# The state-space branch of a decoder trunk: its drive for two state tiles at a time in plain float32, its read-out for four

## The chip, the cores and the metric

The kernel runs on one core of a Trainium2 chip. The metric is the device time of one launch in microseconds (us), as the median of several runs. Engines are named as in the profile: PE is TensorE's matmul stream and PEld its weight loads, DVE is VectorE, ACT is ScalarE, POOL is GpSimd, SP issues the weight DMAs.

## What is computed

Two layers of a decoder trunk on 256 tokens of width 1024, all in float32. Each layer is a SwiGLU feed-forward half step, a mixing step and a second feed-forward half step. The mixing step projects the normed input once; its columns go to a sliding-window attention (3 groups of 8 heads) and to a state-space branch of width 512 (32 groups of 16 channels, 64 complex states a group). Cut to that branch:

```python
u = u.reshape(Bsz, S, SSM_GROUPS, SSM_GROUP)
bu_re = jnp.einsum('bsgc,gpc->bsgp', u, bb_re)      # the drive
bu_im = jnp.einsum('bsgc,gpc->bsgp', u, bb_im)
...
_, _, xr, xi = lax.associative_scan(combine, (ar, ai, bu_re, bu_im), axis=1)
y = (jnp.einsum('bsgp,gcp->bsgc', xr, c_re) - jnp.einsum('bsgp,gcp->bsgc', xi, c_im)
     + d_skip * u)                                   # the read-out and the skip
y = jax.nn.gelu(y.reshape(Bsz, S, SSM_WIDTH))
ga, gb = jnp.split(y @ w_glu, 2, axis=-1)
return ga * jax.nn.sigmoid(gb)
```

## The kernel before

**Weights.** Every large product is done in float32r, in three products of halves: `mm3` (lines 200 to 203) multiplies the high half of a weight (`whi`) with the low and the high half of the data, and its low half (`wlo`) with the high half of the data. The weights come from memory as plain float32 in units of 2048 columns (`raw`, a ring of four, read by SP as a place comes free). `split_one` makes the halves: a cast on ACT (L163) and a subtraction on DVE (L164), up to seven half units ahead of PE (`NHB`). Units of the modulation's weights are spread among them and are multiplied and summed on DVE (L247).

**The mixing step** (`mix_sub`) runs these products in order: a first block of six column tiles; queries and keys for head pairs (`qk`), values (`v`), gates (`gt`), the attention's projection (`ap`), the state-space branch's last projection (`ga`, `gb`), the output (`mo`). After each column tile `tock` runs the work that is due in that slot of a table (`at`): small pieces of attention (logits `lg`, transposes `pt`, outputs `po`) and of the state-space branch. They stand between the large matmuls on PE.

**The state-space branch.** A layer has 16 state tiles of 128 states; four tiles (a quad, `q`) share 128 channels of u, and each tile reads 32 of them. For tile s at its slot m:

- `ssm_in` (slot m - 1), the drive: real and imaginary part, each in three float32r products over 32 rows of the array (`bh` with `ul`, `bh` with `uh`, `bl` with `uh`), 256 columns each, six matmuls into one PSUM bank (`bu`). The row group is 32 times (s mod 4).
- `ssm_turn` (slot m) and `ssm_scan` (m + 1): nine DVE instructions that turn the drive by a table (`tab`), scan it twice over time and turn it back into `xs`.
- `ssm_out` (slot m + 3 of an odd tile), the read-out of tiles s - 1 and s: plain float32, two matmuls a tile (`cw` with `xs`), each tile in its own group of 32 columns, into the bank `yps` of the quad, which is taken with the quad's first pair.
- after a quad: `ssm_skip` adds `d_skip` times u in two DVE steps (for `uh` and `ul`), `ssm_gelu` and `ssm_low` make the halves for the last projection.

Ahead of this, `split_act` makes the halves `bh` and `bl` of B, and `uh`, `ul` are made from the first block's tiles.

**Order.** SP, POOL and ACT run in the order of the code. In the mixing step, behind its first block, PE and DVE are ordered by the framework's scheduler, which moves pieces by its own estimate of when their inputs are ready. All PSUM tiles come from one pool of eight banks (`bank`).

Of the kernel before, what the change touches and what calls it, by code (L numbers as in the profile page):

```python
# [10 lines left out]
F32 = mybir.dt.float32  # L11
# [9 lines left out]
S = 256  # L21
# [42 lines left out]
def plan_units():  # L64
    """Order in which the units of weights are read: ('w', i) or ('a', i)."""
# [22 lines left out]
def ada_chunks(gi):  # L88
    """(layer, chunk of 1024 columns) of the modulation made in group gi."""
# [13 lines left out]
def trunk(ctx, tc, xT, cv, par, ssmp, cst, emat, tbl, wada, wpk, bmat, cmat, out):  # L103
# [37 lines left out]
    def take_ada():  # L141
        """Modulation units whose turn it is."""
# [42 lines left out]
    def several(n):  # L185
        """Halves that are read together."""
# [48 lines left out]
    def ada_unit():  # L235
        """256 columns of silu(c) @ w_ada, one column per partition and element."""
# [57 lines left out]
    def soon(fn):  # L294
        """fn, with its instructions ahead of those that are emitted up to SOON earlier."""
# [16 lines left out]
    def rstd_start():  # L312
        """1 / sqrt(mean of squares + eps), tokens on partitions."""
# [17 lines left out]
    def rstd_spread(ys):  # L331
        """The same on every partition, in PSUM."""
# [169 lines left out]
    def table_side(l, pool):  # L502
        """Cosine and sine of each state's angle over time, for the scans of layer l."""
# [27 lines left out]
    def gate_of(sub):  # L531
        """Half the gate."""
# [71 lines left out]
    def first_block(nx, sj, rj):  # L604
        """Five column tiles of a sublayer's input projection. They read scale * x; the rest read the
        normed chunks, which are made meanwhile. What comes back: the banks, 1 / rms, the normed chunks."""
# [44 lines left out]
    def first_block_whole(nx, sub):  # L651
        """The same for four column tiles, in plain float32."""
        scale, shift, z = nx
        us = [("w", first[sub] + j) for j in range(2)]
        ws = [raw.pop(u).rearrange("p (a b) -> p a b", b=128) for u in us]
        look()
        pss = [bank("b1") for _ in range(4)]

        def mms(ks):
            for j in range(4):  # L660
                for k in ks:
                    T.matmul(pss[j][:, :S + 2], lhsT=ws[j // 2][:, 8 * (j % 2) + k, :], rhs=z[:, k, :],
                             start=k == 0, stop=k == KC - 1)
                if ks[0] == 0 and j == 1:
                    stat_mm()
                    stat["ys"] = rstd_start()
                if ks[0] > 0 and j % 2:
                    finish(us[j // 2])
                    take_ada()

        mms(range(5))
        rps = rstd_spread(stat["ys"])
        rs = tmp.tile([128, S], F32, name="rs", tag="sqa", bufs=1)
        A.copy(out=rs, in_=rps)
        hh, hl = [], []
        for k in h_tiles(rs, scale, shift, hh, hl):
            pass
        mms(range(5, KC))
        look()
        return pss, rs, hh, hl  # L680

    def first_sublayer():
# [183 lines left out]
    def mix_sub(sub, l, nx, close):  # L866
# [5 lines left out]
        if 1:  # L872
# [107 lines left out]
            def ssm_out(s):  # L980
                """State tiles s - 1 and s into their channels."""
                q, jj = divmod(s, 4)
                if jj == 1:
                    yps[q] = bank("yps")
# [398 lines left out]
```

## Time and profile before

| | |
|---|---|
| median of 3 runs | 1366.13 us (1364.47 to 1367.0) |
| span of the profiled execution, first to last instruction | 1361.8 us |
| PE busy | 1322.1 us (97%) |
| DVE busy | 1098.3 us (81%) |
| ACT busy | 757.2 us (56%) |
| mean granted clock of TensorE | 0.993 of full speed |
| DMA | 321.60 MB, mean 236 GB/s |

The profiled execution has no time of its own beside its span; the median stands 4.3 us above it. A busy time is the share of the span in which the engine had an instruction under way. Matmuls overlap: a record lasts longer than the distance to the next one, so PE's work is read from starts, not from durations. One plain float32 matmul shows as two records. `x8` behind a timeline row means eight records of one group that were merged; the row then lasts from the first start to the last end.

### The profile page before, as it was taken

To read this page: it belongs to the slowest core of one execution; us is meant where nothing else is said; L and a number is where in the kernel's file an instruction comes from. 1 tells how busy PE (TensorE), PEld (TensorE's weight loads), DVE (VectorE), ACT (ScalarE), POOL (GpSimd) and SP (SyncE) were. 2 spreads that over 40 slices of the span, in tenths; PEclk is the share of its full clock that TensorE was granted. 3 is DMA by queue.
4 is the path that set the end of the run, shared out by engine and by line. 5 is a ranking of instruction groups with operands and counts; after the bars stand their busy time and mean duration, and the time that the engine had idled before them with its cause. 6 is when DMAs were issued, how large, how long until landed. Compare 5 with 4: busy or idle time off the path is not lost.

```text
span 1361.8 us, 26855 instructions
## 1 busy us (share of the span) xinstructions
PE 1322.1 (97%) x11018; PEld 1279.4 (94%) x11018; DVE 1098.3 (81%) x1757; ACT 757.2 (56%) x1162; POOL 292.6 (21%) x356
## 2 busy tenths in 40 slices
PE   4996999999999999999999999999999999999997
PEld 2996999998988999999999999999889999999997
DVE  8866997889899879998769888679889887876552
ACT  5634795645565456677646444454565645654441
POOL 5889691100000000877300000010000000000000
PEclk9997999999999999999999999999999999999999
DMA  9775997556665645998837988656555463586540
GB/s 356 297 289 175 369 347 274 187 193 207 219 234 219 217 153 170 347 370 321 279 124 291 351 316 333 247 174 227 173 199 198 163 220 128 182 307 217 186 155 32
DMA packets 48837, 321.60 MB, mean 236 GB/s; under 512 B 6048, under 2 KB 6432, under 8 KB 12746
## 3 DMA queue, kind: packets, MB, share of 16 engines
q1 hardware_dynamic: 41704, 296.24, 59.8%
q0 software_dynamic: 7008, 23.64, 5.4%
q8 instruction: 86, 1.41, 0.4%
q14 instruction: 37, 0.30, 0.1%
q10 hardware_dynamic: 2, 0.00, 0.0%
HBM read 310.38 MB, written 9.48 MB: 235 GB/s over the span
## 4 chain that ended last, share of the span: by engine, by line
PE 86%; POOL 6%; DVE 3%; issue 2%; ACT 1%; DMA 1%; DVEq 0%; POOLq 0%; ACTq 0%
PE pc L203 8%; PE pc L201 8%; PE pc L202 8%; PE fo L201 6%; PE fo L202 6%; PE fo L203 6%; PE qk L201 4%; PE qk L202 3%; PE qk L203 3%; PE gt L201 3%; PE gt L202 2%; PE gt L203 2%; PE b L201 2%; PE bu L949 2%; PE b L203 2%; PE b L202 2%
## 5 line engine op out<-in xcount | busy, mean ns | idle before, releaser
L164 DVE TENSOR_TENSOR wlo<-raw,whi 128x1024 fp32r<-128x1024 f32 x416 | 515.5, 1257 | 93.2 <-ACT whi L163 92.3
L163 ACT CAST whi<-raw 128x1024 fp32r<-128x1024 f32 x416 | 427.0, 1047 | 220.2 <-PE fo L202 71.3
L201 PE MATMUL pc<-hl,whi 128*128 128x256 f32 x1200 | 338.4, 282 | 8.7 <-ACT whi L163 8.7
L203 PE MATMUL pc<-hh,wlo 128*128 128x256 f32 x1200 | 338.2, 282 | 3.6 <-DVE wlo L164 3.6
L202 PE MATMUL pc<-hh,whi 128*128 128x256 f32 x1200 | 338.2, 282 | 0.0
L201 PEld LDWEIGHTS pc<-hl,whi 128*128 128x128 f32 x1200 | 226.6, 189 | 8.9 <-ACT whi L163 8.9
L203 PEld LDWEIGHTS pc<-hh,wlo 128*128 128x128 f32 x1200 | 226.5, 189 | 4.1 <-DVE wlo L164 4.1
L202 PEld LDWEIGHTS pc<-hh,whi 128*128 128x128 f32 x1200 | 226.7, 189 | 0.0
L201 PE MATMUL fo<-al,whi 128*128 128x256 f32 x704 | 197.7, 281 | 0.2 <-DVE al L341 0.2
L202 PE MATMUL fo<-ah,whi 128*128 128x256 f32 x704 | 197.8, 281 | 0.0
L203 PE MATMUL fo<-ah,wlo 128*128 128x256 f32 x704 | 197.7, 281 | 0.0
L247 DVE CUSTOM_DVE_ANT_0 raw<-raw,cb 128x1024 f32<-128x1024 f32 x144 | 182.2, 1300 | 7.4 <-DMA raw<-wada 7.1
L201 PEld LDWEIGHTS fo<-al,whi 128*128 128x128 f32 x704 | 132.6, 188 | 0.4 <-DVE al L341 0.4
L202 PEld LDWEIGHTS fo<-ah,whi 128*128 128x128 f32 x704 | 132.7, 188 | 0.0
L203 PEld LDWEIGHTS fo<-ah,wlo 128*128 128x128 f32 x704 | 132.7, 188 | 0.0
L201 PE MATMUL qk<-hl,whi 128*128 128x256 f32 x352 | 102.4, 292 | 0.0
L202 PE MATMUL qk<-hh,whi 128*128 128x256 f32 x352 | 99.1, 282 | 0.0
L203 PE MATMUL qk<-hh,wlo 128*128 128x256 f32 x352 | 98.7, 281 | 0.0
L389 POOL TENSOR_SCALAR tr<-tp 128x256 f32<-128x256 f32 x32 | 45.6, 1424 | 146.8 <-ACT tp L509 146.1
L883 POOL DMA_DIRECT2D tab<-tab x32 | 17.4, 545 | 267.8 <-DVE pq L276 171.3
L201 PE MATMUL gt<-hl,whi 128*128 128x256 f32 x256 | 74.7, 292 | 0.0
L201 PEld LDWEIGHTS qk<-hl,whi 128*128 128x128 f32 x352 | 66.1, 188 | 7.1 <-issue 4.7
(220 smaller groups left out, 2915.4 us busy)
## 6 DMA issues: line engine op xcount, KB each, us to landing
raw<-wpk SPq DMA_DIRECT2D x208, 1024.0 KB, 5.4
raw<-wada SPq DMA_DIRECT2D x72, 1024.0 KB, 6.8
tab<-tb POOLq DMA_DIRECT2D x32, 256.0 KB, 5.7
tab<-tab POOLq DMA_DIRECT2D x32, 256.0 KB, 3.6
bt<-wd POOLq DMA_DIRECT2D x8, 640.0 KB, 6.2
xt<-xT SPq DMA_DIRECT2D x1, 1024.0 KB, 4.9
bT<-bmat POOLq DMA_DIRECT2D x2, 512.0 KB, 4.8
out<-xt SPq DMA_DIRECT2D x4, 256.0 KB, 2.2
```

The costliest lines, as they stand in the source:

```text
L163: A.copy(out=hi.rearrange("p a b -> p (a b)"), in_=src)
L164: low.tensor_sub(out=lo.rearrange("p a b -> p (a b)"), in0=src, in1=hi.rearrange("p a b -> p (a b)"))
L201: T.matmul(ps, lhsT=wh, rhs=hl, start=start, stop=False)
L202: T.matmul(ps, lhsT=wh, rhs=hh, start=False, stop=False)
L203: T.matmul(ps, lhsT=wl, rhs=hh, start=False, stop=stop)
L247: V.tensor_tensor_reduce(out=wj, in0=wj, in1=cb, scale=1.0, scalar=0.0, op0=ALU.mult, op1=ALU.add, accum_out=m[:, c:c + 1])
L389: G.tensor_scalar(out=o, in0=i, scalar1=s1, scalar2=s2, op0=op0, op1=op1)
L883: G.dma_start(out=tabs[s], in_=tabd[l][s])
L949: T.matmul(ps[:, i * S:i * S + S], lhsT=w[r, i, q, :], rhs=u[q][r], start=n == 0, stop=n == 2, tile_position=(32 * jj, 0))
```

## The change

Four things change in `mix_sub`; nothing else does, but for a function that was never called (`first_block_whole`, since `NATIVE` is empty) and comments.

- B is kept in plain float32 (`bT`, a tile of its own), u too (`us`). The halves `bh`, `bl`, `ul` and what makes them are gone.
- The drive runs for tiles s and s + 1 together, at even s: one plain float32 matmul for each part and tile, the two tiles taking turns, so that the row group changes with every matmul. Each tile has its own bank.
- The read-out runs once a quad, at slot m + 3 of its last tile: eight plain float32 matmuls, the four tiles (column groups) taking turns. The scans' outputs `xs` have four buffers instead of two. The bank `yps` is taken only here.
- The skip is one DVE step instead of two.

```diff
-            bT = sp.tile([128, 1024], F32, name="bT", tag="pq", bufs=1)
-            bh, bl = (sp.tile([128, 2, 4, 128], F32R, name=n) for n in ("bh", "bl"))
-            G.dma_start(out=bT, in_=bmat[l].rearrange("p a b c -> p (a b c)"))
-            split_act(bT, bh.rearrange("p a b c -> p (a b c)"), bl.rearrange("p a b c -> p (a b c)"))
+            bT = sp.tile([128, 2, 4, 128], F32, name="bT")
+            G.dma_start(out=bT, in_=bmat[l])
...
                 t, c = first_out(pss.pop(0), rs)
-                a = sp.tile([128, S], F32R, name="uh", tag="uh", bufs=4)
-                b = sp.tile([128, S], F32R, name="ul", tag="ul", bufs=4)
...
-                stt(in_time(b), t, c, in_time(a), AD, SU)
+                a = sp.tile([128, S], F32, name="u", tag="uh", bufs=4)
+                A.activation(out=in_time(a), in_=t.rearrange("p (k m) -> p k m", k=2), func=AF.Identity, bias=c)
+                us.append(a)
...
             def ssm_in(s):
-                q, jj = divmod(s, 4)
-                ps = bank("bu")
-                r = slice(32 * jj, 32 * jj + 32)
+                for n in (s, s + 1):
+                    bus[n] = bank("bu")
                 for i in range(2):
-                    for n, (w, u) in enumerate(((bh, ul), (bh, uh), (bl, uh))):
-                        T.matmul(ps[:, i * S:i * S + S], lhsT=w[r, i, q, :], rhs=u[q][r], start=n == 0, stop=n == 2,
+                    for n in (s, s + 1):
+                        q, jj = divmod(n, 4)
+                        r = slice(32 * jj, 32 * jj + 32)
+                        T.matmul(bus[n][:, i * S:i * S + S], lhsT=bT[r, i, q, :], rhs=us[q][r], start=True, stop=True,
                                  tile_position=(32 * jj, 0))
...
-                x = sp.tile([128, 2, S], F32, name="xs", tag="xs", bufs=2)
+                x = sp.tile([128, 2, S], F32, name="xs", tag="xs", bufs=4)
...
-            def ssm_out(s):
-                q, jj = divmod(s, 4)
-                if jj == 1:
-                    yps[q] = bank("yps")
+            def ssm_out(q):
+                yps[q] = bank("yps")
                 for i in range(2):
-                    for j2 in (jj - 1, jj):
-                        T.matmul(yps[q][32 * j2:32 * j2 + 32, :S], lhsT=cw[:, i, 4 * q + j2, :],
...
+                    for jj in range(4):
+                        T.matmul(yps[q][32 * jj:32 * jj + 32, :S], lhsT=cw[:, i, 4 * q + jj, :],
+                                 rhs=prods[4 * q + jj][:, i], start=i == 0, stop=i == 1, tile_position=(0, 32 * jj))
...
-                stt(yys[q], uh[q], d, yps.pop(q)[:, :S], MU, AD)
-                stt(yys[q], ul[q], d, yys[q], MU, AD)
+                stt(yys[q], us[q], dskip[:, 4 * l + q:4 * l + q + 1], yps.pop(q)[:, :S], MU, AD)
...
-                at(m - 1, ssm_in, s)
+                if s % 2 == 0:
+                    at(m - 1, ssm_in, s)
...
-                if s % 2:
-                    at(m + 3, ssm_out, s)
                 if s % 4 == 3:
+                    at(m + 3, ssm_out, s // 4)
```

How this stands on the engines, in layer 0's mixing step. PE at the first drive, before (L201 to L203 are the large products of `qk`, L1113 to L1115 those of `v`):

```order
L203 MATMUL qk<-hh_3116,wlo 128x256
L949 MATMUL bu<-ul,bh 128x256
L949 MATMUL bu<-uh,bh 128x256
L949 MATMUL bu<-uh,bl 128x256
L949 MATMUL bu<-ul,bh 128x256
L949 MATMUL bu<-uh,bh 128x256
L949 MATMUL bu<-uh,bl 128x256
L1113 MATMUL v<-whi,hl_3034 128x256
```

and after, at the same place:

```order
L202 MATMUL qk<-hh_3116,whi 128x256
L203 MATMUL qk<-hh_3116,wlo 128x256
L913 MATMUL bu<-u,bT 128x256 x4
L1071 MATMUL v<-whi,hl_3034 128x256
L1072 MATMUL v<-whi,hh_3033 128x256
```

Six float32r matmuls of one tile became four plain ones of two tiles; the second tile's own six, 48 large matmuls later, are gone.

PE at a read-out of the first quad, before (one matmul of tile 2 alone, between two halves of the transposes `pt`):

```order
L203 MATMUL qk<-hh_3116,wlo 128x256
L1050 MATMUL pt<-cs,lg 128x128 x4
L987 MATMUL yps<-xs,cw 32x256
L1050 MATMUL pt<-cs,lg 128x128 x4
L1113 MATMUL v<-whi,hl_3034 128x256
```

and after, the read-out of the whole quad:

```order
L203 MATMUL qk<-hh_3116,wlo 128x256
L1008 MATMUL pt<-cs,lg 128x128 x8
L948 MATMUL yps<-xs,cw 32x256 x8
L1071 MATMUL v<-whi,hl_3034 128x256
L1072 MATMUL v<-whi,hh_3033 128x256
```

The quad's matmuls stood in five places on PE before and stand in one now. In each layer, the second quad's are the only ones that are cut, into 3, 2 and 3 by matmuls of `po`.

DVE ahead of the first drive, before (`fo`, `fb` take the first block's tiles out of PSUM):

```order
L276 TENSOR_TENSOR fo<-b_2922,rs 128x256
L787 COPY fb<-b_2922 128x1
L164 TENSOR_TENSOR wlo<-raw,whi 128x1024
L341 TENSOR_TENSOR bl<-bT,bh 128x1024
L279 SCALAR_TENSOR_TENSOR ul<-fo,fb,uh 128x2x128 x3
L276 TENSOR_TENSOR fo<-b_2923,rs 128x256
L787 COPY fb<-b_2923 128x1
```

and after:

```order
L276 TENSOR_TENSOR fo<-b_2922,rs 128x256
L756 COPY fb<-b_2922 128x1
L164 TENSOR_TENSOR wlo<-raw,whi 128x1024
L276 TENSOR_TENSOR fo<-b_2923,rs 128x256
L756 COPY fb<-b_2923 128x1
```

The low halves of B and of u are gone. Further on, DVE has made 123 low halves of weights by the end of the layer's last scan before and after, and 60 products of the modulation where there were 62; in layer 1 it has made 331 low halves where there were 330, and as many products.

## Rows read from the trace of the kernel before

**Rows 1.** the page: busy time, share of the span and instructions of each engine:

```profile
PE 1322.1 (97%) x11018; PEld 1279.4 (94%) x11018; DVE 1098.3 (81%) x1757; ACT 757.2 (56%) x1162; POOL 292.6 (21%) x356
```

**Rows 2.** busy time by stretch: from:to, length, engines' busy time, PEclk, DMA share, GB/s:

```profile
262.00:454.00 192.00, 191.92 (x1611) 174.45 (x1610) 177.26 (x319) 105.52 (x166) 10.95 (x17) 1.00 0.61 212
454.00:540.00 86.00, 86.00 (x715) 84.72 (x714) 69.25 (x134) 48.48 (x79) 0.00 (x0) 1.00 0.51 180
916.00:1107.00 191.00, 190.92 (x1620) 174.92 (x1619) 169.73 (x300) 107.82 (x169) 10.96 (x17) 1.00 0.57 196
```

**Rows 3.** waits of TensorE, longest first: total us, times, longest:

```profile
PE pc L201 <- ACT whi L163: 8.7, 1, 8.7
```

**Rows 4.** groups of instructions: xcount, busy us, mean ns, idle before:

```profile
L987 PE MATMUL yps<-xs,cw 128*32 128x256 f32 x128 | 22.0, 387 | 0.0
...
L949 PE MATMUL bu<-ul,bh 32*128 32x256 f32 x64 | 21.0, 328 | 0.0
```

**Rows 5.** timeline of TensorE around a drive: start, us, line, operation, tiles:

```profile
290.85 0.28 PE L203 MATMUL qk<-hh,wlo 128*128 128x256 f32 x1
291.06 0.38 PE L949 MATMUL bu<-ul,bh 32*128 32x256 f32 x1
...
292.19 0.27 PE L202 MATMUL qk<-hh,whi 128*128 128x256 f32 x1
```

**Rows 6.** timeline of TensorE around two read-outs, of one matmul and of four:

```profile
283.13 0.28 PE L1115 MATMUL v<-wlo,hh 128*128 128x256 f32 x1
283.34 0.62 PE L987 MATMUL yps<-xs,cw 128*32 128x256 f32 x2
...
284.11 0.29 PE L202 MATMUL qk<-hh,whi 128*128 128x256 f32 x1
...
335.06 0.28 PE L1115 MATMUL v<-wlo,hh 128*128 128x256 f32 x1
335.26 1.06 PE L987 MATMUL yps<-xs,cw 128*32 128x256 f32 x8
...
336.48 0.28 PE L202 MATMUL qk<-hh,whi 128*128 128x256 f32 x1
```

**Rows 7.** timeline of TensorE around the logits of a head pair:

```profile
286.73 0.28 PE L203 MATMUL qk<-hh,wlo 128*128 128x256 f32 x1
286.94 1.16 PE L1020 MATMUL lg<-qk 64*128 64x128 f32 x16
...
288.25 0.28 PE L202 MATMUL qk<-hh,whi 128*128 128x256 f32 x1
```

**Rows 8.** groups of instructions on VectorE:

```profile
L247 DVE CUSTOM_DVE_ANT_0 raw<-raw,cb 128x1024 f32<-128x1024 f32 x144 | 182.2, 1300 | 7.4 <-DMA raw<-wada 7.1
...
L279 DVE SCALAR_TENSOR_TENSOR ul<-fo,fb,uh 128x256 fp32r<-128x256 f32 x8 | 3.5, 480 | 0.0
...
L341 DVE TENSOR_TENSOR bl<-bT,bh 128x1024 fp32r<-128x1024 f32 x2 | 2.4, 1223 | 1.6 <-ACT bh L340 1.6
```

**Rows 9.** timelines of VectorE and TensorE at each layer's last scan and read-out:

```profile
452.37 0.75 DVE L276 TENSOR_TENSOR xs<-xs,pq 128x256 f32<-128x256 f32 x2
...
453.64 0.62 PE L987 MATMUL yps<-xs,cw 128*32 128x256 f32 x2
...
456.63 0.63 PE L987 MATMUL yps<-xs,cw 128*32 128x256 f32 x4
...
1101.65 0.75 DVE L276 TENSOR_TENSOR xs<-xs,pq 128x256 f32<-128x256 f32 x2
...
1106.54 1.06 PE L987 MATMUL yps<-xs,cw 128*32 128x256 f32 x8
```

**Rows 10.** waits of VectorE between 262 and 454 us:

```profile
DVE wlo L164 <- ACT whi L163: 3.9, 6, 1.3
DVE yl L1005 <- ACT yh L1001: 2.9, 2, 2.6
```

**Rows 11.** waits of VectorE between 916 and 1107 us:

```profile
DVE pq L276 <- PE bu L949: 6.3, 4, 2.5
```

More of the change, by code (lines that the diff above doesn't have):

```diff
@@ L649, in first_block @@
         return pss, rs, hh, hl
[L651 to L680, printed above, removed]
     def first_sublayer():
@@ L798, in ffn_sub @@
             with tc.manual_schedule(engines={E.PE}):
-                pss, rs, hh, hl = first_block_whole(nx, sub) if sub in NATIVE else first_block(nx, *(J2 if sub % 3 == 2 else J0))
+                pss, rs, hh, hl = first_block(nx, *(J2 if sub % 3 == 2 else J0))
         close()
@@ L867, in mix_sub @@
         with tc.manual_schedule(engines={E.PE}):
-            pss, rs, hh, hl = first_block_whole(nx, sub) if sub in NATIVE else first_block(nx, *(J2 if sub % 3 == 2 else J0))
+            pss, rs, hh, hl = first_block(nx, *(J2 if sub % 3 == 2 else J0))
         close()
@@ L893, in mix_sub @@
             load_bias(0)
-            cT = sp.tile([128, 2, 16, 16], F32, name="cT", tag="xs", bufs=2)
-            ct = sp.tile([128, 2, 16, 16], F32, name="ct", tag="xs", bufs=2)
+            cT = sp.tile([128, 2, 16, 16], F32, name="cT", tag="xs", bufs=4)
+            ct = sp.tile([128, 2, 16, 16], F32, name="ct", tag="xs", bufs=4)
             cw = sp.tile([128, 2, 16, 32], F32, name="cw")
@@ L915, in mix_sub @@
                 ctt(cw[r, 1, :, 16 * g:16 * g + 16], ct[r, 0], ct[r, 1], SU)
-            uh, ul, yh, yl = [], [], [], []
+            us, yh, yl = [], [], []
             for j in range(4):
                 t, c = first_out(pss.pop(0), rs)
-                a = sp.tile([128, S], F32R, name="uh", tag="uh", bufs=4)
-                b = sp.tile([128, S], F32R, name="ul", tag="ul", bufs=4)
-                t = t.rearrange("p (k m) -> p k m", k=2)
-                A.activation(out=in_time(a), in_=t, func=AF.Identity, bias=c)
-                stt(in_time(b), t, c, in_time(a), AD, SU)
-                uh.append(a)
-                ul.append(b)
+                a = sp.tile([128, S], F32, name="u", tag="uh", bufs=4)
+                A.activation(out=in_time(a), in_=t.rearrange("p (k m) -> p k m", k=2), func=AF.Identity, bias=c)
+                us.append(a)
             ev = {}
@@ L942, in ssm_in @@
             def ssm_in(s):
-                q, jj = divmod(s, 4)
-                ps = bank("bu")
-                r = slice(32 * jj, 32 * jj + 32)
+                for n in (s, s + 1):
+                    bus[n] = bank("bu")
                 for i in range(2):
-                    for n, (w, u) in enumerate(((bh, ul), (bh, uh), (bl, uh))):
-                        T.matmul(ps[:, i * S:i * S + S], lhsT=w[r, i, q, :], rhs=u[q][r], start=n == 0, stop=n == 2,
+                    for n in (s, s + 1):
+                        q, jj = divmod(n, 4)
+                        r = slice(32 * jj, 32 * jj + 32)
+                        T.matmul(bus[n][:, i * S:i * S + S], lhsT=bT[r, i, q, :], rhs=us[q][r], start=True, stop=True,
                                  tile_position=(32 * jj, 0))
-                bus[s] = ps
             def ssm_turn(s):
@@ L978, in ssm_scan @@
                 prods[s] = x
-            def ssm_out(s):
-                q, jj = divmod(s, 4)
-                if jj == 1:
-                    yps[q] = bank("yps")
+            def ssm_out(q):
+                yps[q] = bank("yps")
                 for i in range(2):
-                    for j2 in (jj - 1, jj):
-                        T.matmul(yps[q][32 * j2:32 * j2 + 32, :S], lhsT=cw[:, i, 4 * q + j2, :],
-                                 rhs=prods[4 * q + j2][:, i], start=i == 0, stop=i == 1,
-                                 tile_position=(0, 32 * j2))
+                    for jj in range(4):
+                        T.matmul(yps[q][32 * jj:32 * jj + 32, :S], lhsT=cw[:, i, 4 * q + jj, :],
+                                 rhs=prods[4 * q + jj][:, i], start=i == 0, stop=i == 1, tile_position=(0, 32 * jj))
             def ssm_skip(q):
                 yys[q] = tmp.tile([128, S], F32, name="yy", tag="sqa", bufs=1)
-                d = dskip[:, 4 * l + q:4 * l + q + 1]
-                stt(yys[q], uh[q], d, yps.pop(q)[:, :S], MU, AD)
-                stt(yys[q], ul[q], d, yys[q], MU, AD)
+                stt(yys[q], us[q], dskip[:, 4 * l + q:4 * l + q + 1], yps.pop(q)[:, :S], MU, AD)
             def ssm_gelu(q):
```

## The prediction

> **What bounds the kernel now.** I read the page's busy times first, then the same times by stretch, then who waited for whom on TensorE and on VectorE, then the timeline of single visits. TensorE is busy for 97% of the span and VectorE for 81% [rows 1]. By stretch [rows 2], TensorE is full in the mixing sublayers: 191.92 of 192 us in 262 to 454 (layer 0) and 190.92 of 191 in 916 to 1107 (layer 1), at granted clock 1.00, the upper level. But VectorE is at 177.26 of 192 and 169.73 of 191 there: 92% and 89%. So in these stretches, where every edit lies, TensorE sets the pace with VectorE close behind. TensorE's longest wait in the whole run is 8.7 us, for an ACT cast ahead of a feed-forward matmul [rows 3]; in the mixing sublayers it has next to none, by the 0.08 us that are missing [rows 2]. After 454 VectorE is loose again (69.25 of 86), so what TensorE saves before that should reach the end: the weights are read as buffers come free, and move along.
>
> **The price of a visit.** Ordinary float32r matmuls of 256 columns follow one another every 0.12 us (86.00 us for 715) [rows 2]. A drive or read-out uses part of the array, and going in and out of it costs extra. I price a visit from the start of the last ordinary matmul before it to the start of the second one behind it, less two pitches (0.24).
>
> - Drive, before: 292.19 - 290.85 = 1.34, less 0.24, is **1.10 us** for the six matmuls of one state tile [rows 5]. There are 32 visits: each of the three products has 64 records, two a tile [rows 4].
> - Read-out, before: one plain float32 matmul is two records, and costs 284.11 - 283.13 - 0.24 = **0.74**; four matmuls in two column groups (x8) cost 336.48 - 335.06 - 0.24 = **1.18** [rows 6]. The x2 row lasts 0.62 and a record 0.39 [rows 4], so the second starts 0.23 behind the first: a round in line. The x8 row lasts 1.06, so the eighth starts 0.67 behind the first: three rounds of 0.22, not seven. The eight went in four rounds of two. Two column groups do run side by side in plain float32.
> - Logits: eight plain float32 matmuls of 128 columns alternate between two row groups (of 64 rows). Half as wide, each of the 16 records is worth 0.11, and in line they would take 1.8. The whole visit, ways in and out with it, costs 288.25 - 286.73 - 0.24 = **1.28** [rows 7]: eight rounds of two. This is the nearest row for the new drive: plain float32, alternate row groups, 128-column weights.
>
> **The drive, new.** Two tiles are four matmuls, eight records, in two row groups of 32 rows: four rounds. If the groups overlap as the logits' do, a pair costs between 1.18 (the x8 read-out, narrow weights) and 1.28 (the logits, wide ones); I take 1.25, near the logits because of the weights. 16 x 1.25 = 20.0 against 32 x 1.10 = 35.2: **15.2 us less**, 7.6 a layer. The pieces stand together in the new order (four matmuls in a row at all 16 places), so the pairs are not broken up.
>
> The Trainium skill, "FP8 and Floating Point Precision", TensorE Precision Notes, says that true float32 takes four passes through the array. The trace agrees: two records of 0.22 where an ordinary matmul takes 0.12. By that rule alone, without overlap, the edit trades three passes for four; that is the second rival below.
>
> **The read-out, new.** In the old order layer 0 has 16 visits: eight of one matmul, three of two, two of three, three of four. One or two matmuls are two rounds (0.74), three or four are four rounds (1.18): 11 x 0.74 + 5 x 1.18 = 14.0. Layer 1 has three of one, one of two, one of three, six of four: 4 x 0.74 + 7 x 1.18 = 11.2. In the new order each layer has three whole visits of eight matmuls, and one cut into 3, 2 and 3 by the attention's output matmuls. If four column groups overlap, eight matmuls are still four rounds: 3 x 1.18 + 3 x 0.74 = 5.8 a layer, 11.5 in all against 25.2: **13.7 us less**. No row shows four groups, only two; with two at a time each of the eight quads costs four more rounds, 0.88, 7.0 in all, so the gain is bounded by 6.7 and 13.7. I take the upper end: two groups showed no loss at all.
>
> The Trainium skill, "TensorE: Matmul & The Clock Gate", Measured speedup vs the span model, has three column tiles at 2.38 times one, 79% of full. As an estimate from that page, a round would be 0.28 and the 32 new rounds 1.9 us longer: 1342 where I say 1340. No row here shows three or four groups.
>
> **What leaves the other engines.** Per layer: one ACT cast and one VectorE subtraction of 1.22 for the halves of B, four low halves of u at 0.48, four second skip steps of the same size [rows 8]: 5.1 us of VectorE. The ACT cast is worth nothing, since ACT is at 56% [rows 1]. B is then ready straight from its DMA, earlier than now. Scratch grows to four scan outputs, which takes no time of an engine.
>
> **What is late next: VectorE.** The last read-out needs the scan of the layer's last tile. In layer 0 VectorE ends it at 452.37 + 0.75 = 453.1, and the old pieces stand at 453.64 and 456.63 [rows 9]. TensorE would now come there sooner by 7.6 (drive) + 11.8 (the 14.0 without the last pair's three pieces) - 4.6 (the new visits before it) = 14.8: at 438.8. VectorE up to that scan loses 1.22 + 4 x 0.48 + 3 x 0.48, and the new order puts two of the modulation's products (1.30 each [rows 8]) behind it: 7.2 us. If its 14.7 us of idle time stayed, it would end at 445.9 and TensorE would stand 7.1 us; if all of it went, not at all. Of the idle time, 3.9 is for ACT casts that wait for TensorE to free buffers and moves along; 2.9 for a step of ACT stays [rows 10]. In layer 1 the scan ends at 1102.4 [rows 9], and a low half moved ahead of it leaves a loss of 3.4: 1099.0 with the idle time unchanged, against TensorE at 1106.54 - 7.6 - (11.2 - 5.8) = 1093.5: a wait of up to 5.5. But there 6.3 us of VectorE's idle time is a wait for the drive itself [rows 11], which comes sooner. So the waits cost 0 to 12.6 us; I take 3, since the idle time that moves along or shrinks covers most of the lag. The low halves of the weights don't bind before that: TensorE, full as it is, waits for none there today.
>
> **The sum.** 15.2 + 13.7 - 3 = 26 us (25.9). The profiled span is 1361.8, and the median of the runs 1366.13, which I take to be 4.3 us around it, unchanged: 1335.9 and **1340.2 us**.
>
> **The rivals.**
>
> - VectorE takes over. Its idle time stays as it is and the waits of 12.6 are paid: the gain is 16.3 and the time 1350. For it: 92% busy, and scans that ended 3.5 and 4.1 us before the piece that needs them [rows 9]. Against: part of its idle time is TensorE's doing. With checkpoints before the last also late, 1354.
> - Row groups don't overlap for the drive. A pair is then eight rounds, four more than the x8 read-out has: 1.18 + 4 x 0.22 = 2.06, 16 x 2.06 = 33.0, a gain of 2.2 in place of 15.2. TensorE is slower, so VectorE's lag is gone: 1366.1 - 2.2 - 13.7 = 1350. For it: the groups are of 32 rows, which no plain float32 row shows. Against: the logits, eight rounds for 16 records. If column groups go two at a time as well, 1357.
> - Column groups go two at a time: gain 22, lag about 1 us, 1345.
> - Slower: PSUM. A pair takes two of the eight banks at once, and the second is read only when VectorE gets to the next tile, on average 192 / 16 = 12 us later [rows 2]. If TensorE then lacks a bank and stands for VectorE, it decides from 29 / 16 = 1.8 us a pair. A quarter of the 12 us, 3 us at each of 16 pairs, is 48 us: 1366 - 29 + 48 = 1385. Against it: the read-out's bank, now held through half the quad's scans, is then taken only for the last step, so as many bank-times are freed as added; and no wait for a bank shows today.
> - The edit does nothing, because visits are hidden anyway: excluded by a TensorE that is full in both stretches, but for 2 in 100.
>
> **How the numbers follow.** Forecast 1334 to 1344, 60 in 100; column groups in pairs 10; VectorE 14; row groups in line 11; slower 3; nothing 2. The range for 8 in 10 leaves out the worst of VectorE's case, both groups in line, and what is beyond: 1332 to 1352. Its lower end is the sum without any wait (1337) with pairs at 1.18 and visits next to other partial ones paying only one way in. A measurement of this kernel tells about 0.2% from no change; faster by more than that 0.95, within it 0.02, slower 0.03.
>
> **What would show it.** Right: a drive visit of eight records in two row groups at 1.2 to 1.3 us; a read-out visit of sixteen records at about 1.2; TensorE still without gaps in the mixing stretches, shorter by 14 to 17 us in layer 0 and 12 to 14 in layer 1; VectorE above 95% there. Wrong: a drive visit near 2.1 (rounds in line); a read-out near 2.1 (two groups at a time); TensorE idle ahead of the read-out, released by VectorE's scan outputs, by more than 5 us a layer; or TensorE idle ahead of the drive or an ordinary matmul, released by VectorE's reading of a bank.

## The result, and the profile after

| | before | after |
|---|---|---|
| median | 1365.3 us, 4 runs | 1343.99 us (1342.56 to 1345.06, 4 runs) |
| span of the profiled execution | 1361.8 us | 1342.8 us (its own time: 1344.56) |

The ratio is 0.9845, with a 95% interval of 0.9833 to 0.9856: 21.3 us faster by the medians, 19.0 by the spans. The forecast was 1340.2, in a range of 1332 to 1352. So the sign and the range held, and the gain was 5 to 7 us smaller than the 26 of the sum.

The page of after, busy times of the engines, against [rows 1]:

```profile
PE 1297.5 (97%) x10954; PEld 1262.0 (94%) x10954; DVE 1089.7 (81%) x1739; ACT 755.8 (56%) x1160; POOL 292.3 (22%) x356
```

The same by stretch for the two mixing sublayers, against [rows 2] (from:to, length, then busy time of PE, PEld, DVE, ACT, POOL, granted clock, DMA share, GB/s):

```profile
262.00:442.00 180.00, 178.42 (x1580) 165.65 (x1582) 171.19 (x309) 103.64 (x163) 10.97 (x17) 1.00 0.63 220
...
904.00:1088.00 184.00, 181.10 (x1590) 166.83 (x1588) 164.12 (x293) 104.72 (x163) 10.98 (x17) 0.99 0.58 200
```

TensorE, which had been full in both stretches, is now idle for 1.6 and 2.9 us of them, and in layer 1 its clock is no longer 1.00 throughout. VectorE is at 95% in layer 0 and 89% in layer 1.

Timeline of TensorE around a drive pair and around the last read-out of layer 1, to be priced as in [rows 5] and [rows 6]:

```profile
263.14 0.28 PE L203 MATMUL qk<-hh,wlo 128*128 128x256 f32 x1
263.35 1.13 PE L913 MATMUL bu<-u,bT 32*128 32x256 f32 x8
...
264.63 0.29 PE L1072 MATMUL v<-whi,hh 128*128 128x256 f32 x1
...
1086.75 0.28 PE L203 MATMUL ap<-oh,wlo 128*128 128x256 f32 x1
1086.95 1.07 PE L948 MATMUL yps<-xs,cw 128*32 128x256 f32 x16
...
1088.18 0.28 PE L202 MATMUL ap<-oh,whi 128*128 128x256 f32 x1
```

The pair costs 264.63 - 263.14 - 0.24 = 1.25, which is the value taken. The read-out of four column groups, sixteen records, costs 1088.18 - 1086.75 - 0.24 = 1.19: the price of eight records in two groups. Nothing is lost with four. So the new matmuls are as cheap as forecast, and the missing time has to be waits. Waits of TensorE (total us, times, longest) in layer 0 and then in layer 1:

```profile
PE pt L1008 <- ACT lg L1001: 1.0, 1, 1.0
PE yps L948 <- DVE xs L276: 0.5, 1, 0.5
PE gb L201 <- DVE yl L963: 0.3, 1, 0.3
...
PE yps L948 <- DVE xs L276: 1.4, 1, 1.4
PE pt L1008 <- ACT lg L1001: 1.4, 2, 1.0
```

To see what each sublayer gained, free of what differs elsewhere, I take the distance from the first `qk` matmul of a layer to its first `mo` matmul, which all kernels have. (Spans are a poorer measure: in these executions the first `qk` starts anywhere from 250.7 to 254.6 us, behind code that is the same.)

(Sums are taken before rounding.)

| kernel | layer 0, us | layer 1, us | gained on before |
|---|---|---|---|
| before | 235.85 | 232.98 | |
| after | 223.17 | 225.68 | 12.7 + 7.3 = 20.0 |
| drive alone | 225.58 | 227.26 | 10.3 + 5.7 = 16.0 |
| drive of single tiles | 230.59 | 229.84 | 5.3 + 3.1 = 8.4 |
| neighbours in the same group | 223.21 | 224.89 | 12.6 + 8.1 = 20.7 |
| four tiles in the drive | 224.11 | 227.14 | 11.7 + 5.8 = 17.6 |
| cT first | 223.82 | 221.42 | 12.0 + 11.6 = 23.6 |
| one sum on POOL | 227.30 | 225.79 | 8.6 + 7.2 = 15.8 |
| light after | 222.41 | 222.46 | 13.4 + 10.5 = 24.0 |
| light before | 233.64 | 233.64 | 2.2 - 0.7 = 1.6 |
| late transposes | 220.65 | 220.65 | 15.2 + 12.3 = 27.5 |
| late read-outs | 220.16 | 219.64 | 15.7 + 13.3 = 29.0 |

Between the mixing sublayers the shift stays at what layer 0 gave it: nothing is given back in the feed-forward sublayers. After gained 12.7 and 7.3 us, where the visits alone should have given 15.8 and 13.1. The 9 us between are the subject of the experiments. One thing has to be watched in this table: the scheduler puts TensorE's small pieces together differently in some of the kernels, so a row can gain or lose by that as well. Where it matters, I sum the prices of the visits themselves.

Layer 1 has the larger hole, and it opens in the first read-out. Timeline of VectorE at the start of that layer:

```profile
910.08 0.43 DVE L870 TENSOR_TENSOR ct<-cT,fre 128x256 f32<-128x256 f32 x1 [5.68 <-DMA cT<-cmat]
```

POOL's, which issues the loads:

```profile
897.49 0.55 POOL L864 DMA_DIRECT2D cT<-cmat  x1
```

The same two in the kernel before:

```profile
919.14 0.43 DVE L903 TENSOR_TENSOR ct<-cT,fre 128x256 f32<-128x256 f32 x1 [0.68 <-DMA cT<-cmat]
...
909.76 0.55 POOL L897 DMA_DIRECT2D cT<-cmat  x1
```

TensorE's at the first read-out, 40 us later:

```profile
947.38 0.63 PE L948 MATMUL yps<-xs,cw 128*32 128x256 f32 x6
949.44 1.91 PE L948 MATMUL yps<-xs,cw 128*32 128x256 f32 x10 [1.42 <-DVE xs L276]
```

Busy times and granted clock by stretch, from there on:

```profile
949.00:951.00 2.00, 1.56 (x10) 0.55 (x10) 1.91 (x5) 0.00 (x0) 0.00 (x0) 0.62 0.93 225
951.00:953.00 2.00, 2.00 (x9) 1.72 (x9) 1.97 (x5) 0.00 (x0) 0.00 (x0) 0.53 0.63 209
```

VectorE stands 5.68 us for cT, the tile of the read-out's weights, whose load is issued last on POOL's queue; before it stood 0.68. Two things make up the 5.0 us between. VectorE no longer splits B and u, so it is ready for cT 6.9 us after the load's issue (910.08 - 5.68 - 897.49) where it took 8.7 before (919.14 - 0.68 - 909.76): 1.8. And the load itself lands 12.6 us after its issue (910.08 - 897.49) where it took 9.4: 3.2. In that time SP issues two loads of weights (at 901.0 and 903.3), where before it issued one (at 917.3). No run tests whether these slow cT's load.

With that lag the scan is late for the read-out: TensorE issues three matmuls (x6), stands 1.42 us, and then has a mean granted clock of 0.62 and 0.53 in the next two stretches of 2 us, so it runs most of them at the lower level, 1.2 GHz.

### The profile page after: what moved, and what is told of

It is laid out like the page before. It is cut to its first block, busy times and chain, and to the rows that moved or that the text cites. A ratio compares the mean times of both kernels' runs of the same rounds, so it can differ in the third digit from the quotient of the medians.

```text
span 1342.8 us, 26704 instructions
## 1 busy us (share of the span) xinstructions
PE 1297.5 (97%) x10954; PEld 1262.0 (94%) x10954; DVE 1089.7 (81%) x1739; ACT 755.8 (56%) x1160; POOL 292.3 (22%) x356
## 5 line engine op out<-in xcount | busy, mean ns | idle before, releaser
L201 PE MATMUL pc<-hl,whi 128*128 128x256 f32 x1200 | 338.2, 282 | 8.7 <-ACT whi L163 8.7
L203 PE MATMUL pc<-hh,wlo 128*128 128x256 f32 x1200 | 338.2, 282 | 3.7 <-DVE wlo L164 3.7
L201 PEld LDWEIGHTS pc<-hl,whi 128*128 128x128 f32 x1200 | 226.6, 189 | 8.9 <-ACT whi L163 8.9
L203 PEld LDWEIGHTS pc<-hh,wlo 128*128 128x128 f32 x1200 | 226.4, 189 | 4.1 <-DVE wlo L164 4.1
L201 PE MATMUL fo<-al,whi 128*128 128x256 f32 x704 | 197.7, 281 | 1.1 <-DVE al L341 1.1
L203 PE MATMUL fo<-ah,wlo 128*128 128x256 f32 x704 | 197.7, 281 | 0.0
L201 PEld LDWEIGHTS fo<-al,whi 128*128 128x128 f32 x704 | 132.6, 188 | 1.3 <-DVE al L341 1.3
L203 PEld LDWEIGHTS fo<-ah,wlo 128*128 128x128 f32 x704 | 132.7, 188 | 0.0
L201 PE MATMUL qk<-hl,whi 128*128 128x256 f32 x352 | 100.8, 287 | 0.0
L203 PE MATMUL qk<-hh,wlo 128*128 128x256 f32 x352 | 98.7, 281 | 0.0
L201 PE MATMUL gt<-hl,whi 128*128 128x256 f32 x256 | 74.1, 289 | 0.0
L340 ACT CAST ah<-mu 128x512 fp32r<-128x512 f32 x44 | 27.1, 617 | 80.0 <-DVE mu L814 71.9
L202 PE MATMUL gt<-hh,whi 128*128 128x256 f32 x256 | 72.2, 282 | 0.0
```

What stands on the lines that cost most here:

```text
L201: T.matmul(ps, lhsT=wh, rhs=hl, start=start, stop=False)
L202: T.matmul(ps, lhsT=wh, rhs=hh, start=False, stop=False)
L203: T.matmul(ps, lhsT=wl, rhs=hh, start=False, stop=stop)
L340: A.copy(out=hi, in_=src)
```

## The experiments

Two theories stood at the start. Theory 1: the visits save what was forecast, 29 us, and the rest went into waits behind VectorE. Theory 2: the visits save less than their own starts show, and no wait matters.

**The drive alone.** The new drive, with the old read-out and its slots (and `xs` in two buffers again):

```
...
-                if s % 4 == 3:
-                    at(m + 3, ssm_out, s // 4)
+                if s % 2:
+                    at(m + 3, ssm_out, s)
...
```

> The drive of the changed kernel (pairs, plain float32) with the read-out of the kernel before (pieces of one or two state tiles as they become ready). Theory 1, the visits cost what the forecast said (pairs 1.25 us, 15.2 us less TensorE work in all) and what is missing from the forecast is waits behind VectorE: VectorE loses about 6 us a layer here and TensorE 7.6, so next to no new waits: before less 13 to 15 us, 1350 to 1352. Theory 2, no waits matter and the new visits save less than they seem to by their own starts (the ordinary matmuls beside them pay): about 21/29 of 15.2, so before less 11 us, 1354 to 1355. The read-out then accounts for the rest of the changed kernel's 21 us.

1349.47 us, ratio 0.9887 (0.9872 to 0.9902): 16.0 us in the mixing sublayers, a shade above theory 1's 15.2. That the two are so near is partly chance: the old read-outs did not keep their places. The scheduler put them into 20 visits where there were 27, which by their starts cost 21.8 us where they cost 25.6, and one of them waits 1.7 for the scan. What the drive paid is read from its visits: 16 at 1.25. For the read-out, 10.7 were then left to gain (21.8 - 11.1), and the changed kernel added only 4.0 (20.0 - 16.0): the waits ate the rest.

**The drive of single tiles.** Plain float32 with one tile to a visit, at the old places:

```
-                for n in (s, s + 1):
+                for n in (s,):
...
-                if s % 2 == 0:
-                    at(m - 1, ssm_in, s)
+                at(m - 1, ssm_in, s)
```

> The changed kernel with the drive in plain float32 for one state tile at a time, at the old places: two matmuls, four records, all in one row group, 32 visits. Nothing can run beside anything. If rounds in one row group go in line as those of the read-out of one matmul do (0.74 for two records, 0.22 for each more): 1.18 a visit, 32 x 1.18 = 37.8 against 20.1 for the pairs, 17.7 us more TensorE work. VectorE's lag is then gone and its waits with it (theory 1): 9 to 13 us slower than the changed kernel, 1353 to 1357; with no waits to win back (theory 2) 1361.

1356.32 us, ratio 0.9938 (0.9921 to 0.9954). Timeline of a visit:

```profile
263.75 0.28 PE L203 MATMUL qk<-hh,wlo 128*128 128x256 f32 x1
263.96 1.13 PE L913 MATMUL bu<-u,bT 32*128 32x256 f32 x4
...
265.24 0.29 PE L1071 MATMUL v<-whi,hh 128*128 128x256 f32 x1
```

One tile costs 265.24 - 263.75 - 0.24 = 1.25: what two cost side by side. The second tile of a pair is free. Sixteen more visits are 20 us of TensorE work, yet only 11.6 of them show (20.0 - 8.4): with a slower TensorE the waits of the changed kernel all but go. That speaks for theory 1. The only wait left on TensorE in the mixing sublayers is the one for the softmax, half as long each time as in the changed kernel:

```profile
PE pt L1008 <- ACT lg L1001: 0.9, 2, 0.5
```

**Neighbours in the same group.** The same matmuls, written so that neighbours mostly share a row group, and two column groups before the other two:

```
-                for i in range(2):
-                    for n in (s, s + 1):
+                for n in (s, s + 1):
+                    for i in range(2):
...
-                for i in range(2):
-                    for jj in range(4):
+                for jp in (0, 2):
+                  for i in range(2):
+                    for jj in (jp, jp + 1):
```

> The changed kernel with the same matmuls in another order inside each visit: a drive pair does both products of one state tile, then both of the other (neighbours in the same row group), and a read-out does two column groups, then the other two. If neighbours in different groups are what overlaps: a drive visit of 1.9 to 2.1 us instead of 1.26 and a read-out of 1.9 to 2.1 instead of 1.20, so 16 x 0.8 + 8 x 0.8 = 19 us more TensorE work. Theory 1 (9 us of the changed kernel are waits behind VectorE, which a slower TensorE no longer has): only 10 to 15 us slower than the changed kernel, 1354 to 1359. Theory 2 (no waits matter): the whole 19 us, 1363. If the order of neighbours does not matter, 1344.

1343.97 us, ratio 0.9853 (0.9837 to 0.9869): no difference from the changed kernel. Both theories missed, since both took for granted that neighbours must alternate. Timeline of a drive:

```profile
262.86 0.28 PE L203 MATMUL qk<-hh,wlo 128*128 128x256 f32 x1
263.07 1.14 PE L913 MATMUL bu<-u,bT 32*128 32x256 f32 x8
...
264.36 0.29 PE L1073 MATMUL v<-whi,hh 128*128 128x256 f32 x1
```

The price is 1.26. The eight records still start in four rounds of two, 14 ns apart inside a round where they were 6 to 7 ns apart before. A whole read-out is 1.20 or 1.21 where nothing waits, instead of 1.19, still four rounds and not eight; only the one that attention's matmuls cut in three costs 0.8 more, since its first and its last piece now each put two matmuls in one group. The overlap needs matmuls of different groups in one visit, not an alternating order.

**Four tiles in the drive.** Eight visits in place of sixteen, in four row groups:

```
-                for n in (s, s + 1):
+                for n in range(s, s + 4):
...
-                if s % 2 == 0:
+                if s % 4 == 0:
```

> The changed kernel with the drive for four state tiles at a time in four row groups, 8 visits instead of 16, each taking four of the eight banks at once. If four row groups overlap as four column groups do, a visit of sixteen records still takes about 1.26 and TensorE's work falls by 8 x 1.26 = 10 us. Theory of a TensorE that sets the pace alone: 1334 to 1336. Theory 1 (VectorE, at 95% of the layer 0 stretch, sets it): most of the 10 us become waits, 1341 to 1345. The rival with banks (a bank held until VectorE reads it makes TensorE wait): three banks a visit held for 12, 24 and 36 us; waits of TensorE released by VectorE's reading of the drive, slower than the changed kernel, 1350 or more.

1348.68 us, ratio 0.988 (0.9865 to 0.9895). Timeline of a visit:

```profile
263.65 0.28 PE L203 MATMUL qk<-hh,wlo 128*128 128x256 f32 x1
263.85 1.15 PE L913 MATMUL bu<-u,bT 32*128 32x256 f32 x16
...
265.15 0.29 PE L1072 MATMUL v<-whi,hh 128*128 128x256 f32 x1
```

TensorE's waits from 255 to 1120 us:

```profile
PE pt L1008 <- ACT lg L1001: 6.6, 3, 3.0
PE yps L948 <- DVE pq L276: 4.2, 2, 3.7
PE v L1071 <- DVE pq L276: 1.2, 1, 1.2
PE lg L978 <- DVE pq L276: 1.0, 1, 1.0
```

Four tiles cost 265.15 - 263.65 - 0.24 = 1.26: TensorE's work falls by 10 us. And the kernel is slower, 17.6 gained instead of 20.0. New among the waits are those of `yps`, `v` and `lg`, which TensorE writes, released by VectorE's `pq`, the step that reads a drive's bank: `v` and `lg` take nothing else from that step, so they wait for a bank. The rival that I held at 3 in 100 is thus real at four banks a visit. The changed kernel, with two, shows no such wait.

**cT's load first.** The line moves ahead of B, the tables and the bias on POOL's queue; TensorE's order is the same:

```
...
+            G.dma_start(out=cT, in_=cmat[l])
             bT = sp.tile([128, 2, 4, 128], F32, name="bT")
             G.dma_start(out=bT, in_=bmat[l])
...
-            G.dma_start(out=cT, in_=cmat[l])
             G.memset(cw, 0.0)
```

> The changed kernel with the load of the read-out's weights (cT) issued on POOL's queue ahead of B, the three tables and the bias, in place of behind them; TensorE's order is the same. Theory 1 (VectorE's 5.7 us stop for cT in layer 1 is what makes the first read-out there wait 1.9 us, stretches that stretch of work by a fall of the granted clock, and delays the transposes): the stop is gone or under 1 us, the first read-out of layer 1 waits under 0.5 us, granted clock 1.0 throughout, 3 to 4 us faster than the changed kernel: 1340 to 1341. Rival (the stop is made up for anyway, or the tables come late in its place): 1343 to 1345.

1340.86 us, ratio 0.9827 (0.9813 to 0.9842). By medians that is 3.1 us under the changed kernel, and the two intervals overlap a little; the stretches tell it better. Layer 1 takes 221.42 where it took 225.68, 4.3 us less: VectorE has no wait for cT there any more and TensorE none for the first read-out. POOL in layer 1:

```profile
879.45 0.54 POOL L846 DMA_DIRECT2D cT<-cmat  x1 [222.88 <-DVE sq L292]
897.69 0.54 POOL L848 DMA_DIRECT2D bT<-bmat  x1 [17.70 <-PE b L203]
```

So the move is worth far more than a place in the queue: B's load waits on POOL for TensorE's first block, cT's does not, and it now goes out 18.2 us ahead of B's.

Layer 0, where the changed kernel already had cT early, is 0.7 us longer. TensorE's waits from 255 to 1120 us:

```profile
PE pt L1008 <- ACT lg L1001: 2.1, 2, 1.0
PE yps L948 <- DVE xs L276: 1.4, 1, 1.4
```

The transposes (`pt`) still wait, and layer 0's third read-out waits longer.

**One sum of each state tile on POOL.**

```
-                tt(x[:, 1], x[:, 1], p1[:, 0], AD)
+                G.tensor_tensor(out=x[:, 1], in0=x[:, 1], in1=p1[:, 0], op=AD)
```

> The changed kernel with one of VectorE's eight steps a state tile (the sum for the imaginary part of the scan's output, 0.37 us) done by POOL: 16 x 0.37 = 6 us a layer less for VectorE, 12 in all; POOL has 0.96 us for a tile of that size. TensorE's order is the same. Theory 1 (TensorE waits behind VectorE's lag in the mixing sublayers): the waits for the transposes in front of attention's products (1.4 us each) and for the read-outs shrink, 2 to 5 us faster than the changed kernel, 1339 to 1342. Theory 2 (TensorE alone sets the time): 1344, or a little slower where POOL's longer step delays a read-out.

1353.08 us, ratio 0.9908 (0.9888 to 0.9929), 9 us slower than the changed kernel: both theories missed. The step on POOL, and the one that stayed on VectorE, as groups of this kernel:

```profile
L940 POOL TENSOR_TENSOR xs<-xs,pq 128x256 f32<-128x256 f32 x32 | 38.9, 1215 | 277.5 <-DVE pq L276 105.1 <-DVE st L1000 62.7 <-DVE xs L276 60.2
...
L276 DVE TENSOR_TENSOR xs<-xs,pq 128x256 f32<-128x256 f32 x32 | 18.6, 580 | 0.1
```

VectorE's two as they are in the changed kernel:

```profile
L276 DVE TENSOR_TENSOR xs<-xs,pq 128x256 f32<-128x256 f32 x64 | 24.2, 419 | 0.1
```

POOL takes 1215 ns, and VectorE's own sum beside it grows from 419 to 580. The Trainium skill, "SBUF — State Buffer", "SBUF: two separate sides", says that VectorE and GpSimd share a port pair as an exclusive lock; the 580 agrees with that: the eight of VectorE's sums that overlap none of POOL's take 415 on average, the 24 that do 636. VectorE's two sums took 24.2 us and the one left takes 18.6, and its whole busy time fell only from 1089.7 to 1089.1 us, where 12 was meant. The tables and the bias, loaded from POOL's queue, also stand behind these steps. TensorE's wait for the softmax is 6.7 us in five places, where it was 2.4 in three. The profiled execution was the fastest of four (1348.38), so 5 us of the difference are in no trace and stay open. The relief was no relief.

**VectorE made light.** Two kernels, before and after, without the last two sums of each state tile:

```
-                tt(x[:, 0], x[:, 0], p1[:, 1], SU)
-                tt(x[:, 1], x[:, 1], p1[:, 0], AD)
```

> The kernel before without the last two of VectorE's steps a state tile (the sums that finish the rotation back; the read-out takes what stands there, so the output is another): 16 x 0.75 = 12 us a layer less for VectorE. All theories: TensorE is full in the mixing sublayers of the kernel before, so next to nothing changes: 1363 to 1366. It is the other half of the next run.

> The changed kernel without the same two steps of VectorE: 12 us a layer less for VectorE, so that it is never behind. Theory 1 (TensorE's saving is 29 us as forecast, and about 8 us of the changed kernel are waits behind VectorE): the waits for transposes and read-outs in the mixing sublayers all but vanish, and the time is 26 to 29 us under the light kernel before: 1336 to 1339. Theory 2 (the visits save 21 us and VectorE is not the cause): 1343 to 1344. In between, if cT's late load alone accounts for the waits in layer 1: its stop is in this kernel too, so 1339 to 1341.

1363.43 us (ratio 0.999, 0.998 to 0.9999) and 1341.8 us (0.9831, 0.9817 to 0.9846). The difference is 21.6 us, not 26 to 29; and 22.4 by the stretches. (The light kernel before has its read-outs in 22 visits instead of 27, which accounts for the 1.6 us that it gains on before.) TensorE's waits in the light kernel after, layer 0 and then layer 1:

```profile
PE pt L1006 <- ACT lg L999: 1.0, 1, 1.0
PE gb L201 <- DVE yl L961: 0.7, 1, 0.7
...
PE pt L1006 <- ACT lg L999: 1.7, 2, 1.0
```

VectorE's lag did make the read-outs wait: with 12 us a layer less for VectorE, `yps` waits no more, though VectorE still stands 5.7 us for cT. But the transposes wait as before. So waits eat the gain, as theory 1 has it, and lightening VectorE by these two steps removes only a part of them.

ACT's timeline ahead of the transposes in layer 0, in the changed kernel:

```profile
328.86 1.05 ACT L163 CAST whi<-raw 128x1024 fp32r<-128x1024 f32 x1 [4.23 <-PE v L1072]
...
333.47 1.33 ACT L1001 ACTIVATE lg<-lg,st 128x512 f32<-128x512 f32 x2 [0.47 <-DVE st L1000]
```

VectorE's reciprocal, for which ACT waits the 0.47, and TensorE's there:

```profile
333.28 0.22 DVE L1000 RECIPROCAL st<-st 128x1 f32<-128x1 f32 x2
...
332.92 0.28 PE L203 MATMUL qk<-hh,wlo 128*128 128x256 f32 x1
334.25 1.27 PE L1008 MATMUL pt<-cs,lg 128*128 128x128 f32 x8 [1.05 <-ACT lg L1001]
```

The same place in the kernel before, ACT:

```profile
333.83 1.05 ACT L163 CAST whi<-raw 128x1024 fp32r<-128x1024 f32 x1 [5.45 <-PE v L1114]
...
337.87 0.72 ACT L1043 ACTIVATE lg<-lg,st 128x512 f32<-128x512 f32 x1
```

and TensorE:

```profile
339.20 1.04 PE L1050 MATMUL pt<-cs,lg 128*128 128x128 f32 x8
```

ACT works in order, and a weight cast stands ahead of the exponentials. It waits until TensorE has freed a weight buffer. Behind it come a table load (1.28), the exponentials, the reciprocal on VectorE and the scaling, and then the transposes can start. Before, the first half was scaled at 338.59 (337.87 + 0.72), 4.8 us after the cast's start, and TensorE came for it at 339.20, 5.4 us after it: 0.6 us to spare. A read-out of 1.18 was among what TensorE did meanwhile [rows 6]. Now the read-out stands elsewhere and TensorE is there 1.2 us sooner after the cast. By that alone it would wait some 0.6, and in the run with the drive of single tiles, where ACT has no wait for VectorE at this place, it stands 0.5 each time.

The rest is VectorE's. In the changed kernel its reciprocal stands behind a subtraction of weights and a product of the scan, ACT waits 0.47 for it, and TensorE stands 1.05. The light kernels do not take this away: the two steps that they leave out are not ahead of the reciprocal there, and ACT's wait for it is 0.47 in the light kernel after too. So each of these waits is about half the lost read-out and half VectorE's lag. The next run's theory A holds the first for all of it, theory B the second.

**Late transposes.** With cT first, and the transposes and what follows them one slot later:

```
-                        at(x + 3 + n, fn, p, qt)
-                at(x + 8, att_out, p)
+                        at(x + 3 + n + (n > 1), fn, p, qt)
+                at(x + 9, att_out, p)
```

> The changed kernel with cT's load first (as in the run of that name) and, besides, each head pair's transposes, their eviction, the products with v and the output step one slot later in the hand-written order, so that TensorE has about 3 us of other work more between freeing a weight buffer and needing the softmax. Theory A (the 1.3 us waits at two transposes are a chain through ACT's queue: a cast that waits for TensorE to free a weight buffer stands ahead of the exponentials, and the visits that were taken out no longer cover the chain): both waits vanish, 2.5 to 3 us faster than with cT's load first alone: 1337.5 to 1338.5. Theory B (VectorE's lag makes them): VectorE's order hardly changes, so it is late elsewhere and the time stays within 1 us: 1340 to 1341.

1337.98 us, ratio 0.9806 (0.9793 to 0.9819): theory A's number, 2.9 us under the run with cT first alone. The two waits are gone, but a later slot gives ACT and VectorE time alike, so the run does not part the theories. Nor is its number the two waits' alone (by the stretches the gain is 3.9 us). By starts these cost 1.4 each in the run with cT first (2.3 a visit of transposes, 0.87 where nothing waits), 2.9 together; the wait of layer 0's third read-out, 2.0, went too; TensorE's pieces stand together in other places (the second quad's read-out is no longer cut), which saves 2.8; and new waits cost 3.4. TensorE's longest wait between 255 and 1120 us is now this:

```profile
PE yps L948 <- DVE pq L276: 3.2, 2, 1.8
```

In layer 0, VectorE and then TensorE:

```profile
394.39 0.42 DVE L276 TENSOR_TENSOR xs<-xs,pq 128x256 f32<-128x256 f32 x1
...
396.06 1.22 DVE L276 TENSOR_TENSOR pq<-bu,tab 128x1024 f32<-128x1024 f32 x1
...
397.33 1.07 PE L948 MATMUL yps<-xs,cw 128*32 128x256 f32 x16 [1.82 <-DVE pq L276]
```

The scan's output is complete at 394.8. The read-out starts 2.5 us later, behind the step that reads a drive's bank, and takes nothing else from that step. So this is the wait for a bank again, now at two banks a visit, and in layer 1 it is the same (1.4).

**Late read-outs.** Besides, the first three read-outs of each layer one slot later, with the steps behind them:

```
-                    at(m + 3, ssm_out, s // 4)
-                    at(m + 4, ssm_skip, s // 4)
+                    at(m + 3 + (s < 15), ssm_out, s // 4)
+                    at(m + 4 + (s < 15), ssm_skip, s // 4)
...
```

> As the run with late transposes, and the first three read-outs of each layer one slot later as well, with the steps behind them (the last stays, since what follows needs it). If read-outs wait for VectorE's scan (0.8 us in the changed kernel, 1.7 with cT's load first, at the third read-out of layer 0): that wait is gone and the time 1 to 2 us lower than with late transposes alone: 1336 to 1337. If VectorE's lag only moves on to the last read-out, the same time as that run, with a new wait of 1 us or more ahead of the last read-out.

1336.41 us (1334.54 to 1336.58, 5 runs), ratio 0.9792 (0.9778 to 0.9805): the best kernel here, 27.9 us under the one before by the medians, though its interval and that of the run with late transposes overlap. The waits for a bank are gone too, and the second quad's read-out is cut again. TensorE in the two mixing stretches:

```profile
262.00:442.00 180.00, 180.00 (x1606) 167.80 (x1606) 173.65 (x311) 104.90 (x164) 10.00 (x16) 1.00 0.65 224
904.00:1080.00 176.00, 176.00 (x1575) 163.97 (x1572) 162.21 (x288) 102.03 (x160) 10.01 (x16) 1.00 0.61 206
```

TensorE is full again, at a granted clock of 1.00, with VectorE at 173.65 of 180 (96%), and the two sublayers gain 15.7 and 13.3 us, next to the 15.8 and 13.1 of the forecast's visits. (Its order of pieces is worth 0.9 us more than the changed kernel's, and a wait of 0.3 us ahead of `gb` is left, so the tenths are chance.)

## Why the prediction was right, and where it was not

- **What bounds:** right. What TensorE saved in the mixing sublayers came through to the end unchanged.
- **The drive, 15.2:** right. A pair is 1.25, as taken, at all 16 places. (The 16.0 that the drive alone gained hold 3.8 of read-outs that were put together.) The argument from the logits held; that the groups alternate in the logits had nothing to do with it.
- **The read-out, 13.7:** the visits are right, 1.19 for sixteen records in four column groups (1.18 taken), and the whole 29.0 shows once the waits are out. The 1.9 us more that I had estimated from the Trainium skill, "TensorE: Matmul & The Clock Gate", Measured speedup vs the span model, did not come: four groups lose nothing in these records.
- **The waits, 3:** the step that failed. They were 9.0 us (29.0 - 20.0). They did not stand where I looked, ahead of the last read-out: VectorE reached that in time, within 0.14 us in layer 0, and also in the last kernel, where TensorE is full. They stood at other places. By starts, in the changed kernel itself, they come to 8.8:
  - The first read-out of layer 1, 4.2 with the clock in it. I called B ready earlier than now and counted VectorE's work that goes, but did not ask what VectorE would then meet. The next load on the same queue had 0.9 us or less of waiting before, and 5.7 after. With cT first the layer took 4.3 less.
  - The transposes, 2.9. I put ACT down as loose, at 56%, though its queue is in order and part of its waiting is for TensorE. A read-out of 1.18 had covered the softmax with 0.6 us to spare; it moved away, and VectorE's reciprocal came 0.5 late as well.
  - The third and the last read-out of layer 0, 1.2, for VectorE's scan.
  - `gb` in layer 0, 0.5, for VectorE's last step of the state-space branch. The last kernel has it too.
- **From span to time:** 4.3 us between span and median was too much. In the runs with both it is about 2 (1344.56 against 1342.8), so some 2.3 of it were before's profiled execution being faster than its median. By luck this hid a part of the miss: with 2 us the forecast would have been 1338, and with the waits at 9.0 as well 1343.9, which is the measured time.
- **The rivals:** VectorE taking over, at 12.6, was the right direction: the waits cost 9.0, and only about half of the softmax's part was not VectorE's doing. Row groups in line and column groups in pairs are out. The bank rival does not act in the changed kernel. It does at four banks a visit, and at two once the transposes are moved.
- **The signs:** both visits came out as I said they would if I was right; a TensorE without gaps, and stretches shorter by 14 to 17 and 12 to 14, did not. Of the signs of being wrong none came to its size: TensorE stood for the scan's outputs, but 0.5 and 1.4 us a layer and not 5.

## What to carry to other kernels

Where an engine is full, price the work that is taken from it by starts, then walk through each other engine's queue in order and ask what stands in front of the piece that will now be asked for sooner: a load issued last, or a cast that waits for a buffer. A wait that was covered, here with 0.6 us to spare, does not show in the trace of before; the distance from its releaser to its use does. The repairs then are cheap, three moves in the order of work, and they were worth 7.6 us here by the medians, more than a third of the change itself. What each of them was worth alone is less sure, since each also moved other pieces: after every move, look again at what stands together and at who waits.

## What the runs showed of the hardware

- Two tiles in two row groups, or four in four, cost what one costs, 1.25 to 1.26 us, in plain float32; four column groups cost what two do, 1.19 against 1.18.
- Matmuls of different groups overlap without alternating in the program. With both products of a tile written before those of the other, each pair of starts is still 14 ns apart, so the second group's first matmul starts ahead of the first group's second. Over a whole read-out it cost 0.01 to 0.02 us.
- A PSUM bank that waits for VectorE to read it can hold TensorE up at two banks a visit as at four: 1.8 and 1.4 us with late transposes.
- TensorE's clock can fall after a short wait: to 0.53 here, behind a stand of 1.42 us. It did not fall behind a longer one: with late transposes, TensorE stood 1.82 us, was busy for 0.67 of the 2 us from 396 to 398, and the granted clock stayed at 1.00. No run here settles what decides.
